# First stage of a one-core gMLP trunk: new load order, one chain of sums per tile, columns in one step

## The chip, the cores and the metric

The kernel runs on one core of one Trainium2 chip. The metric is the device time of one execution in microseconds (us); lower is better. A time of the profile is counted from the start of its span. TensorE is PE in the rows (PEld is its weight load), VectorE is DVE, ScalarE is ACT, GpSimd is POOL and SyncE, whose queue issues the DMAs, is SP.

## What is computed

The reference, for one sequence x of 2048 positions and 1024 channels and one conditioning vector c of 1024 (depth 1, expansion to 2048 channels):

```python
mod = silu(c) @ ada_w + ada_b                      # ada_w: 1024 x 3072
shift, scale, gate = split(mod, 3)
h = rmsnorm(x, norm_g) * (1.0 + scale) + shift
u, v, z = split(h @ w_in, 3)                       # each 2048 channels
u = gelu(u); v = layernorm(gelu(v), ln_g, ln_b)
v = einsum("hpq,bnqhc->bnphc", sp_w, v in chunks of 128) + sp_b
y = (u * v * silu(z)) @ w_out
out = rmsnorm(x + gate * y, final_g)
```

## The kernel before

Every large product is made of fp32r halves: an operand is split into hi (a copy rounded to fp32r, ACT, line 168) and lo (operand minus hi, DVE, line 169), and a product is three matmuls, hi·hi, hi·lo and lo·hi (mm3, lines 177 to 180). Sequences go in two blocks of 1024 positions; within a block the large products follow Strassen's scheme with seven half products p1 to p7, whose left sides are S[A11] to S[S4].

The change touches only the **first stage** (lines 723 to 831). It makes the normalised, modulated and transposed input of the first 512 positions, a1[0] to a1[7] (128 channels by 512 positions each), and multiplies it at once by the first columns of w_in: step k takes a1[k], splits it into sh and sl, and makes 18 matmuls of 128x512 into six PSUM banks: four row chunks of v (with ws[k][0], 512 columns) and two tiles of u (ws[k][1]). Steps 0 to 3 accumulate p1, steps 4 to 7 accumulate p2; between them the six banks are copied out by ACT (lines 489 and 326). All later stages follow this one on TensorE.

To modulate a1[k] the stage needs two columns per k, mscale and mshift. They come from ada_w: mod_load(j) (line 209) loads 128 columns of the shift part and 128 of the scale part as one tile aw of 128 x 2 x 8 x 128 values (1 MB, two DMAs of 512 KB, in pieces of 512 bytes), in three rotating buffers. mod_sum(j) (line 218) multiplies its eight k-slices by the eight columns of silu(c) (c_act) and adds them up in **two accumulators** am[:, 0] and am[:, 1], taken in turn: the first product of each is made by DVE (j = 0) or ACT (other j, line 225), six multiply-adds by DVE (line 229), and one more add brings the two together (line 232). Two matmuls with a column of ones then sum over the partitions (line 235, pm), and mod_cols (line 240) makes mscale and mshift with three small DVE instructions.

Ahead of the steps stands a **start**: SP loads c, norm_g and ada_b as rows (lines 724 to 731), then aw 0 and aw 1, then four chunks of x (512 KB each, lines 257 to 264), then wf 0 and wf 1 (the first w_in tiles, lines 272 to 282), aw 2 and wf 2. TensorE turns the rows into columns (line 733); ACT makes c_act (line 734). Each chunk of x is normalised: ACT squares and sums it (line 157), DVE makes the mean r_m (line 149), POOL its power (line 150), DVE multiplies (line 160); TensorE transposes it (line 782). In between TensorE runs products of the identity that nobody reads (spin, lines 751 to 754). Then a1[0] is modulated (line 253) and split, and the first product follows.

The order on DVE and ACT is the written one in the start and in the steps (manual_schedule, lines 769 and 791); TensorE's order is written in the start only, and left to the scheduler in the steps. In step k the program loads aw and wf of k+3, sums aw of **k+2**, modulates and splits a1[k], makes the columns of k+1, multiplies, and splits the weights of k+1 (lines 792 to 831): the sums run two steps ahead of their use. In step 4 it also loads the second half of x and two tiles for the next stage (lines 796 to 799).

## Time and profile before

| | |
|---|---|
| three timed runs | 1334.1, 1338.95, 1339.69 us; median 1338.95 |
| the profiled execution | 1334.47 us, of which its span is 1332.7 us |
| busy share of the span | PE 99%, DVE 81%, ACT 51%, POOL 2% |
| mean granted TensorE clock | 0.999 |
| first product of the steps | 22.06 us after the start of the span |
| last product of step 7 | at 59.91 us; the next stage's first product at 60.14 us |

The span is the time between the first and the last instruction; some 1.8 us of the execution lie around it. A busy PE is not a PE at its peak: matmuls are pipelined, and their ends are modelled.

### The profile page before, as it was taken

The numbers are of one execution on the slowest core, as the hardware profiler recorded it, in microseconds if no ns is written. First come the engines' busy times: TensorE is split into PE (matmuls) and PEld (weight loads), VectorE is DVE, ScalarE is ACT, GpSimd is POOL, SyncE is SP. The second block draws the span as 40 slices with busy tenths as digits, with TensorE's granted clock in tenths as the row PEclk, the third lists the DMA queues.
The fourth block names the chain that finished last, engine by engine and source line by source line (L and its number), as shares of the span: only waits on it lengthen the run. The fifth ranks groups of instructions, "written<-read, shape, count | busy, mean of one in ns | idle before, by whom it ended". The sixth has DMA issues, their size and how long they took to land.

```text
span 1332.7 us, 17438 instructions
## 1 busy us (share of the span) xinstructions
PE 1317.3 (99%) x6174; PEld 1097.6 (82%) x6174; DVE 1077.3 (81%) x1801; ACT 683.6 (51%) x1177; POOL 26.0 (2%) x42
## 2 busy tenths in 40 slices
PE   8999999999999999999999999999999999999997
PEld 7878887888888888788888888888888888888886
DVE  7889988888888988978678889887789944757975
ACT  5875454766755537634355545444544424344453
POOL 0000001000000000000000000000000000000101
PEclk9999999999999999999999999999999999999999
DMA  9871655555565648442243344433339622235723
GB/s 310 293 259 56 232 187 190 179 193 186 198 225 186 216 151 278 165 135 104 102 164 107 112 167 174 152 117 119 125 126 319 248 99 100 103 121 212 244 103 127
DMA packets 156800, 229.26 MB, mean 172 GB/s; under 512 B 9188, under 2 KB 91172, under 8 KB 153384
## 3 DMA queue, kind: packets, MB, share of 16 engines
q1 hardware_dynamic: 156712, 228.14, 50.1%
q8 instruction: 48, 0.79, 0.2%
q14 instruction: 40, 0.33, 0.1%
HBM read 160.47 MB, written 67.64 MB: 171 GB/s over the span
## 4 chain that ended last, share of the span: by engine, by line
PE 87%; DVE 6%; DMA 2%; issue 1%; ACT 1%; POOL 1%; SPq 0%; POOLq 0%; DVEq 0%; ACTq 0%
PE p_u L180 7%; PE p_u L179 7%; PE p_u L178 7%; PE p_z L179 7%; PE p_z L180 7%; PE p_z L178 7%; PE po L180 7%; PE po L179 7%; PE po L178 7%; PE p_v L178 6%; PE p_v L180 6%; PE p_v L179 6%; PE pmix_u L557 4%; DVE lo_p_v L169 1%; PE p L180 1%
## 5 line engine op out<-in xcount | busy, mean ns | idle before, releaser
L178 PE MATMUL p_v<-hi_p_v,sh 128*128 128x512 f32 x416 | 162.5, 391 | 1.9 <-DVE c_v L485 1.0
L180 PE MATMUL po<-hi_o,gl 128*128 128x512 f32 x416 | 162.1, 390 | 0.3 <-DVE gl L169 0.2
L179 PE MATMUL p_v<-lo_p_v,sh 128*128 128x512 f32 x416 | 162.3, 390 | 0.0
L180 PE MATMUL p_v<-hi_p_v,sl 128*128 128x512 f32 x416 | 162.2, 391 | 0.0
L178 PE MATMUL po<-hi_o,gh 128*128 128x512 f32 x416 | 161.8, 389 | 0.0
L179 PE MATMUL po<-lo_o,gh 128*128 128x512 f32 x416 | 161.8, 389 | 0.0
L168 ACT ACTIVATE gh<-gr 128x1024 fp32r<-128x1024 f32 x52 | 55.0, 1060 | 128.3 <-PE po L179 118.3
L168 ACT ACTIVATE hi_p_v<-b_v 128x512 fp32r<-128x512 f32 x104 | 64.9, 630 | 106.3 <-PE p_v L180 87.7
L169 DVE TENSOR_TENSOR gl<-gr,gh 128x1024 fp32r<-128x1024 f32 x52 | 63.5, 1221 | 59.8 <-ACT gh L168 59.7
L169 DVE TENSOR_TENSOR lo_p_v<-b_v,hi_p_v 128x512 fp32r<-128x512 f32 x104 | 69.7, 685 | 36.1 <-ACT hi_p_v L168 35.8
L178 PEld LDWEIGHTS p_v<-hi_p_v,sh 128*128 128x128 f32 x416 | 78.1, 188 | 19.5 <-DVE c_v L485 1.8
L180 PEld LDWEIGHTS po<-hi_o,gl 128*128 128x128 f32 x416 | 78.1, 188 | 17.2 <-DVE gl L169 1.1
L178 PEld LDWEIGHTS po<-hi_o,gh 128*128 128x128 f32 x416 | 78.1, 188 | 16.3
L179 PEld LDWEIGHTS po<-lo_o,gh 128*128 128x128 f32 x416 | 78.1, 188 | 16.2
L179 PEld LDWEIGHTS p_v<-lo_p_v,sh 128*128 128x128 f32 x416 | 78.1, 188 | 16.1 <-DVE lo_p_v L169 0.2
L180 PEld LDWEIGHTS p_v<-hi_p_v,sl 128*128 128x128 f32 x416 | 78.1, 188 | 16.0
L542 ACT ACTIVATE vn<-vn,lm,lr 128x256 f32<-128x256 f32 x128 | 67.7, 590 | 22.4 <-DMA vn<-v_dram 17.1
L180 PE MATMUL p_u<-sh,lo_p_u 128*128 128x512 f32 x196 | 76.3, 389 | 0.0
L178 PE MATMUL p_u<-sh,hi_p_u 128*128 128x512 f32 x196 | 76.3, 389 | 0.0
L179 PE MATMUL p_u<-sl,hi_p_u 128*128 128x512 f32 x196 | 76.2, 389 | 0.0
L180 PE MATMUL p_z<-sh,lo_p_z 128*128 128x512 f32 x192 | 75.0, 391 | 0.0
L178 PE MATMUL p_z<-sh,hi_p_z 128*128 128x512 f32 x192 | 74.7, 389 | 0.0
(248 smaller groups left out, 3113.0 us busy)
## 6 DMA issues: line engine op xcount, KB each, us to landing
gr<-g_dram SPq DMA_DIRECT2D x26, 1024.0 KB, 4.9
b_v<-in_gm_w_in_dram SPq DMA_DIRECT2D x18, 1024.0 KB, 7.5
vn<-v_dram SPq DMA_DIRECT2D x16, 1024.0 KB, 6.0
raw_u<-in_gm_w_in_dram SPq DMA_DIRECT2D x16, 1024.0 KB, 5.3
raw_z<-in_gm_w_in_dram SPq DMA_DIRECT2D x16, 1024.0 KB, 5.0
v_dram<-c_v SPq DMA_DIRECT2D x44, 256.0 KB, 2.1
g_dram<-c_u SPq DMA_DIRECT2D x37, 256.0 KB, 2.7
aw<-in_ada_w_dram SPq DMA_DIRECT2D x16, 512.0 KB, 5.4
```

Of the source, the lines that this page charges most:

```text
L168: nc.scalar.activation(hi, src, AF.Copy)
L169: nc.vector.tensor_tensor(lo, src, hi.bitcast(F32), op=ALU.subtract)
L178: nc.tensor.matmul(ps, lhsT=sh, rhs=mh, start=first, stop=False)
L179: nc.tensor.matmul(ps, lhsT=sh, rhs=ml, start=False, stop=False)
L180: nc.tensor.matmul(ps, lhsT=sl, rhs=mh, start=False, stop=last)
L542: nc.scalar.activation(vt[:, ch, :], vt[:, ch, :], AF.Identity, bias=lm[:, ch:ch + 1], scale=lr[:, ch:ch + 1],)
L557: nc.tensor.matmul(pm[:, i * P:(i + 1) * P], lhsT=vt[:, m * (NCH // 2) + i, f * P:(f + 1) * P], rhs=spT[:, u.j, :], start=True, stop=True,)
```

## The change

The rows are loaded behind aw 0, and x between aw 0 and aw 1; wf 0 comes ahead of aw 1. The sums of a tile run in one accumulator (one add on the other in place), the first product on ACT except for j = 1. The 1 of "1 + scale" is added once to all columns; mscale is then one DVE instruction, and mshift moves to ACT. The order is written out for three engines (DVE, ACT and PE) through the steps: in step k TensorE makes 8 products (13 in step 0), the column of k+1, four transposes (steps 1 to 3) and the other products; DVE adds the last four slices of aw k+1 (six in step 0) and the first three of aw k+2; ACT makes the upper halves of the weights of k+1 before it modulates a1[k+1]. All of a1[1] to a1[4] are copied by ACT. Spins: 6, 13, 3, 5, 4, 3, 6 and, in step 0, 5 more (before: 20, 16, 3, 3, 6).

```diff
@@ -215,38 +215,40 @@
             nc.sync.dma_start(aw[:, s], ada_v[:, :, s * D + j * P:s * D + (j + 1) * P])
         return aw
 
-    def mod_sum(j, aw):
-
-
-        am = s_slot(A22, j % KH, "hl"[j // KH], F32, f"am_{j}", (P, 2, 2, P))
-        for k in range(KD):
-            a, ck = am[:, k % 2], c_act[:, k:k + 1]
-            if k < 2 and j:
-                nc.scalar.activation(a, aw[:, :, k, :], AF.Copy, scale=ck)
-            elif k < 2:
-                nc.vector.tensor_scalar(a, aw[:, :, k, :], ck, None, op0=ALU.mult)
-            else:
-                nc.vector.scalar_tensor_tensor(a, aw[:, :, k, :], ck, a, op0=ALU.mult, op1=ALU.add)
-            if k in (3, 5, 6):
-                yield None
-        nc.vector.tensor_tensor(am[:, 0], am[:, 0], am[:, 1], op=ALU.add)
+    def mod_tile(j):
+        return s_slot(A22, j % KH, "hl"[j // KH], F32, f"am_{j}", (P, 2, P))
+
+    def mod_begin(j, aw, am):
+
+        ck = c_act[:, 0:1]
+        if j == 1:
+            nc.vector.tensor_scalar(am, aw[:, :, 0, :], ck, None, op0=ALU.mult)
+        else:
+            nc.scalar.activation(am, aw[:, :, 0, :], AF.Copy, scale=ck)
+
+    def mod_add(aw, am, ks):
+        for k in ks:
+            nc.vector.scalar_tensor_tensor(
+                am, aw[:, :, k, :], c_act[:, k:k + 1], am, op0=ALU.mult, op1=ALU.add
+            )
+
+    def mod_column(j, am):
+
         pm = aux_bank(f"pm_{j}")
         for s in (1, 0):
             nc.tensor.matmul(
-                pm[:, s:s + 1], lhsT=am[:, 0, s, :], rhs=ones[:, 0:1], start=True, stop=True
+                pm[:, s:s + 1], lhsT=am[:, s, :], rhs=ones[:, 0:1], start=True, stop=True
             )
-        yield pm
+        return pm
 
     def mod_cols(cols, j, pm):
-        nc.vector.tensor_tensor(
-            mscale[:, j:j + 1], pm[:, 1:2], cols[:, R_SC + j:R_SC + j + 1], op=ALU.add
+
+        nc.vector.tensor_scalar(
+            mscale[:, j:j + 1], pm[:, 1:2], cols[:, R_SC + j:R_SC + j + 1],
+            cols[:, R_G + j:R_G + j + 1], op0=ALU.add, op1=ALU.mult,
         )
-        nc.vector.tensor_scalar(
-            mscale[:, j:j + 1], mscale[:, j:j + 1], 1.0, cols[:, R_G + j:R_G + j + 1],
-            op0=ALU.add, op1=ALU.mult,
-        )
-        nc.vector.tensor_tensor(
-            mshift[:, j:j + 1], pm[:, 0:1], cols[:, R_SH + j:R_SH + j + 1], op=ALU.add
+        nc.scalar.activation(
+            mshift[:, j:j + 1], pm[:, 0:1], AF.Identity, bias=cols[:, R_SH + j:R_SH + j + 1]
         )
 
     def modulate(out, src, k):
@@ -281,8 +283,18 @@
         )
         return wv, wu
 
-    def first_split(k, raws):
-        return split_w(raws[0], f"wfv_{k}", (P, FB)), split_w(raws[1], f"wfu_{k}", (P, NF, P))
+    def first_upper(k, raws):
+
+        ws = []
+        for raw, shape, name in zip(raws, ((P, FB), (P, NF, P)), ("wfv", "wfu")):
+            hi = whp.tile(list(shape), F32R, tag="hi", name=f"hi_{name}_{k}")
+            lo = wlp.tile(list(shape), F32R, tag="lo", name=f"lo_{name}_{k}")
+            nc.scalar.activation(hi, raw, AF.Copy)
+            ws.append((hi, lo))
+        return ws
+
+    def first_lower(w, raw):
+        nc.vector.tensor_tensor(w[1], raw, w[0].bitcast(F32), op=ALU.subtract)
 
 
     class Unit:
@@ -721,74 +733,120 @@
     NU = len(units) // NB
 
     with tc.tile_pool(name="start", bufs=1) as st:
+        aws, wf, pm, am = {}, {}, {}, {}
+        aws[0] = mod_load(st, 0)
         nc.sync.dma_start(rows[R_C:R_C + KD, :], c.rearrange("o (k p) -> (o k) p", p=P))
-        nc.sync.dma_start(
-            rows[R_G:R_G + KD, :], norm_g.rearrange("o (k p) -> (o k) p", p=P)
-        )
         nc.sync.dma_start(
             rows[R_SH:R_SH + 2 * KD, :],
             ada_b[:, 0:2 * D].rearrange("o (k p) -> (o k) p", p=P),
         )
-        ps_r = aux_bank("ps_rows")
-        nc.tensor.transpose(ps_r[:, :NR], rows[:NR, :], ident[:NR, :NR])
-        nc.scalar.activation(c_act, ps_r[:, R_C:R_C + KD], AF.Silu)
-        nc.vector.tensor_copy(cols, ps_r[:, :NR])
-
-        aws, wf, pm = {}, {}, {}
-        for k in range(2):
+        nc.sync.dma_start(
+            rows[R_G:R_G + KD, :], norm_g.rearrange("o (k p) -> (o k) p", p=P)
+        )
+        xh = load_half(st, 0)
+        wf[0] = first_load(0)
+        for k in (1, 2):
             aws[k] = mod_load(st, k)
-        xh = load_half(st, 0)
-        for k in range(3):
-            if k == 2:
-                aws[k] = mod_load(st, k)
             wf[k] = first_load(k)
-        a1, first = [], []
+        a1, first, ws = [], [], {}
         firsts = [units[2 * j] for j in range(NF)]
         v0, v1 = groups[0]
-
         spun = acc_bank("spun")
 
-        def spin(n):
+        def spin(n, spun=spun):
 
             for _ in range(n):
                 nc.tensor.matmul(spun[:, :P], lhsT=ident, rhs=ident, start=True, stop=True)
 
...
+        def a1_tile(k):
+            a1.append(s_slot(S4, k % KH, "hl"[k // KH], F32, f"a1_{k}"))
+            return a1[k]
+
+        def upper(k):
+
+            if k:
+                modulate(a1[k], a1[k], k)
             else:
-                nc.scalar.activation(t, ps, AF.Copy)
-            a1.append(t)
-
-        written = {mybir.EngineType.DVE, mybir.EngineType.Activation}
-        with tc.manual_schedule(engines=written | {mybir.EngineType.PE}):
-            spin(20)
-            *_, pm[0] = mod_sum(0, aws[0])
+                modulate(a1_tile(0), psx[0], 0)
+            i, kk = (A11 if k < KH else A12), k % KH
+            hi, lo = [s_slot(i, kk, p, F32R, f"s{p}_0_{i}_{kk}") for p in "hl"]
+            S[i][kk] = (hi, lo)
+            nc.scalar.activation(hi, a1[k], AF.Copy)
+
+        def lower(k):
+            hi, lo = S[A11 if k < KH else A12][k % KH]
+            nc.vector.tensor_tensor(lo, a1[k], hi.bitcast(F32), op=ALU.subtract)
+
+        def products(k):
+            sh, sl = S[A11 if k < KH else A12][k % KH]
+            edges = k % KH == 0, k % KH == KH - 1
+            mm = []
+            for ch in range(4):
+                cs = slice(ch * P, (ch + 1) * P)
+                hi, lo = ws[k][0]
+                mm += [(first[ch], sh[:, cs], hi), (first[ch], sh[:, cs], lo),
+                       (first[ch], sl[:, cs], hi)]
+            for j in range(NF):
+                hi, lo = ws[k][1]
+                ps = first[4 + j]
+                mm += [(ps, hi[:, j], sh), (ps, hi[:, j], sl), (ps, lo[:, j], sh)]
+            for n, (ps, left, right) in enumerate(mm):
+                nc.tensor.matmul(
+                    ps, lhsT=left, rhs=right, start=edges[0] and n % 3 == 0,
+                    stop=edges[1] and n % 3 == 2,
+                )
+                yield
+
+        def some(steps, n):
+            for _ in range(n):
+                next(steps, None)
+
+        engines = {
+            mybir.EngineType.DVE, mybir.EngineType.Activation, mybir.EngineType.PE
+        }
+        with tc.manual_schedule(engines=engines):
+            spin(6)
+            ps_r = aux_bank("ps_rows")
+            nc.tensor.transpose(ps_r[:, :NR], rows[:NR, :], ident[:NR, :NR])
+            nc.scalar.activation(c_act, ps_r[:, R_C:R_C + KD], AF.Silu)
+            nc.vector.tensor_copy(cols, ps_r[:, :NR])
+            nc.vector.tensor_scalar(
+                cols[:, R_SC:R_SC + KD], cols[:, R_SC:R_SC + KD], 1.0, None, op0=ALU.add
+            )
+            spin(13)
+            norm = [normalize_steps(xt, f"0_{ch}") for ch, xt in enumerate(xh)]
+            am[0] = mod_tile(0)
+            mod_begin(0, aws[0], am[0])
+            mod_add(aws[0], am[0], range(1, 5))
+            next(norm[0])
+            mod_add(aws[0], am[0], range(5, KD))
+            next(norm[0])
+            pm[0] = mod_column(0, am[0])
             mod_cols(cols, 0, pm[0])
-            sums = mod_sum(1, aws[1])
+            next(norm[1])
+            next(norm[1])
+            next(norm[2])
+            next(norm[2])
+            ws[0] = first_upper(0, wf[0])
+            first_lower(ws[0][0], wf[0][0])
+            next(norm[3])
+            first_lower(ws[0][1], wf[0][1])
+            next(norm[3])
             psx = [acc_bank(f"psx_0_{k}") for k in range(5)]
             for ch, xt in enumerate(xh):
-                spin((16, 3, 3, 0)[ch])
-                norm = normalize_steps(xt, f"0_{ch}")
-                next(norm)
-                pm[1] = next(sums)
-                next(norm)
+                spin((3, 5, 4, 3)[ch])
                 for k in range(5):
                     nc.tensor.transpose(
                         psx[k][:, ch * P:(ch + 1) * P], xt[:, k * P:(k + 1) * P], ident
                     )
             spin(6)
-            ws = [first_split(k, wf[k]) for k in range(2)]
-            for k in range(5):
-                take_a1(k, psx[k])
-                if k == 0:
-                    put(0, A11, 0, a1[0])
-        with tc.manual_schedule(engines=written):
+            upper(0)
+            am[1] = mod_tile(1)
+            mod_begin(1, aws[1], am[1])
+            mod_add(aws[1], am[1], range(1, 2))
+            lower(0)
+            for k in range(1, 5):
+                nc.scalar.activation(a1_tile(k), psx[k], AF.Copy)
             for k in range(KD):
                 if k + 3 < KD:
                     aws[k + 3] = mod_load(st, k + 3)
@@ -797,38 +855,40 @@
                     x2 = load_half(st, 1)
                     v1.load(0, 0, "raw0")
                     v1.load(1, 0, "raw1")
+                if k % KH == 0:
+                    first = [acc_bank(f"p{k // KH + 1}_{j}") for j in range(4 + NF)]
+                mm = products(k)
+                some(mm, 8 if k else 13)
+                if k + 1 < KD:
+                    mod_add(aws[k + 1], am[k + 1], range(4 if k else 2, KD))
+                    ws[k + 1] = first_upper(k + 1, wf[k + 1])
+                    first_lower(ws[k + 1][0], wf[k + 1][0])
+                    pm[k + 1] = mod_column(k + 1, am[k + 1])
                 if k + 2 < KD:
-                    sums = mod_sum(k + 2, aws[k + 2])
-                    if k < 4:
-                        next(sums)
-                if k:
-                    modulate(a1[k], a1[k], k)
-                i = A11 if k < KH else A12
-                if k:
-                    put(0, i, k % KH, a1[k])
+                    am[k + 2] = mod_tile(k + 2)
+                    mod_begin(k + 2, aws[k + 2], am[k + 2])
+                if 0 < k < KH:
+                    ps = transpose_half(xh, 0, KH + k, aux_bank)
+                for _ in mm:
+                    pass
                 if k + 1 < KD:
                     mod_cols(cols, k + 1, pm[k + 1])
+                    first_lower(ws[k + 1][1], wf[k + 1][1])
+                    if k == 0:
+                        spin(5, aux_bank("spun_1"))
+                if k + 2 < KD:
+                    mod_add(aws[k + 2], am[k + 2], range(1, 4))
+                if k + 1 < KD:
+                    upper(k + 1)
                 if 0 < k < KH:
-                    take_a1(KH + k)
-                if k + 2 < KD:
-                    *_, pm[k + 2] = sums
-                if k == KH:
+                    nc.scalar.activation(a1_tile(KH + k), ps, AF.Copy)
+                if k + 1 == KH:
                     for ch in range(4):
                         v0.evict("p1", ch, first[ch])
                     for j in range(NF):
                         firsts[j].first(first[4 + j], None)
-                if k % KH == 0:
-                    first = [acc_bank(f"p{k // KH + 1}_{j}") for j in range(4 + NF)]
-                sh, sl = S[i][k % KH]
-                edges = k % KH == 0, k % KH == KH - 1
-                for ch in range(4):
-                    cs = slice(ch * P, (ch + 1) * P)
-                    mm3(first[ch], sh[:, cs], sl[:, cs], *ws[k][0], *edges)
-                for j in range(NF):
-                    hi, lo = ws[k][1]
-                    mm3(first[4 + j], hi[:, j], lo[:, j], sh, sl, *edges)
-                if 0 < k < KD - 1:
-                    ws.append(first_split(k + 1, wf[k + 1]))
+                if k + 1 < KD:
+                    lower(k + 1)
         right = [v1.weights("p1", k) for k in range(2)]
         for ch in range(4):
             v0.evict("p2", ch, first[ch])
```

## Rows read from the trace of the kernel before

**Rows 1.** The page: busy time of PE, and the chain that ended last.

```profile
PE 1317.3 (99%) x6174; PEld 1097.6 (82%) x6174; DVE 1077.3 (81%) x1801; ACT 683.6 (51%) x1177; POOL 26.0 (2%) x42
...
PE 87%; DVE 6%; DMA 2%; issue 1%; ACT 1%; POOL 1%; SPq 0%; POOLq 0%; DVEq 0%; ACTq 0%
```

**Rows 2.** Windows: steps 0, 1, 4, 7; length, busy us per engine, PEclk, DMA, GB/s.

```profile
core 0: us, PE busy (x) PEld busy (x) DVE busy (x) ACT busy (x) POOL busy (x), PEclk, DMA share, GB/s
22.00:28.05 6.05, 5.58 (x29) 4.14 (x29) 5.96 (x17) 4.02 (x9) 0.00 (x0) 1.00 1.00 300
28.05:33.09 5.04, 5.04 (x29) 4.21 (x28) 4.97 (x14) 3.67 (x7) 0.00 (x0) 1.00 1.05 313
...
42.80:47.35 4.55, 4.55 (x23) 3.85 (x22) 3.66 (x10) 4.52 (x10) 0.00 (x0) 1.00 1.03 410
...
56.06:60.14 4.08, 4.08 (x20) 3.38 (x18) 3.20 (x6) 3.19 (x5) 0.00 (x0) 1.00 0.41 159
```

**Rows 3.** Timeline of SP: start, length, issue, in the first 10 us.

```profile
0.74 0.40 SPq L724 DMA_DIRECT2D rows<-in_c_dram  x1
...
1.90 3.77 SPq L215 DMA_DIRECT2D aw<-in_ada_w_dram  x4
5.71 3.31 SPq L262 DMA_DIRECT2D x<-in_x_dram  x4
```

**Rows 4.** Windows of 1 us: the last figure is GB/s moved.

```profile
6.00:7.00 1.00, 1.00 (x7) 1.00 (x6) 0.00 (x0) 0.00 (x0) 0.00 (x0) 1.00 1.12 337
...
12.00:13.00 1.00, 1.00 (x12) 1.00 (x11) 0.00 (x0) 0.95 (x1) 0.00 (x0) 1.00 1.03 422
```

**Rows 5.** Timeline, 3 to 13 us: start, length, instruction, [idle before it].

```profile
3.15 0.28 PE L733 MATMUL ps_rows<-ident,rows 32*128 32x32 f32 x1 [3.15 <-DMA rows<-in_ada_b_dram]
...
3.36 7.34 PE L754 MATMUL spun<-ident 128*128 128x128 f32 x40
3.65 0.18 ACT L734 ACTIVATE c_act<-ps_rows 128x8 f32<-128x8 f32 x1
...
7.26 0.61 DVE L227 TENSOR_SCALAR am<-aw,c_act 128x256 f32<-128x256 f32 x2 [3.21 <-DMA aw<-in_ada_w_dram]
7.79 2.46 DVE L229 SCALAR_TENSOR_TENSOR am<-aw,c_act,am 128x256 f32<-128x256 f32 x6
...
10.28 0.42 DVE L232 TENSOR_TENSOR am<-am 128x256 f32<-128x256 f32 x1
...
10.76 0.61 PE L235 MATMUL pm<-ones,am 128*128 128x1 f32 x4
...
11.23 3.82 PE L754 MATMUL spun<-ident 128*128 128x128 f32 x32
11.40 0.16 DVE L241 TENSOR_TENSOR mscale<-pm,cols 128x1 f32<-128x1 f32 x1 [0.70 <-PE pm L235]
...
12.05 1.06 ACT L157 ACTIVATE sq<-x 128x1024 bf16<-128x1024 f32 x1 [8.23 <-DMA x<-in_x_dram]
```

**Rows 6.** Timeline, 13 to 23 us: chunks 0 and 3 of x, the first product.

```profile
13.24 0.15 DVE L149 TENSOR_SCALAR r_m<-ss 128x1 f32<-128x1 f32 x1 [1.36 <-ACT sq L157]
...
18.41 0.15 DVE L149 TENSOR_SCALAR r_m<-ss 128x1 f32<-128x1 f32 x1
...
19.39 0.75 DVE L160 TENSOR_SCALAR x<-x,r 128x1024 f32<-128x1024 f32 x1
...
22.06 0.49 PE L178 MATMUL p<-hi_wfv,sh 128*128 128x512 f32 x1
```

**Rows 7.** Timeline of DVE and ACT in the steps, 30 to 42 us.

```profile
30.81 0.80 ACT L253 ACTIVATE a<-a,mshift,mscale 128x512 f32<-128x512 f32 x1
30.89 0.69 DVE L169 TENSOR_TENSOR lo_wfv<-wfv,hi_wfv 128x512 fp32r<-128x512 f32 x1
...
31.49 0.42 DVE L169 TENSOR_TENSOR lo_wfu<-wfu,hi_wfu 128x256 fp32r<-128x256 f32 x1
...
31.64 0.63 ACT L168 ACTIVATE sh<-a 128x512 fp32r<-128x512 f32 x1
...
41.89 2.04 ACT L489 ACTIVATE c_v<-p 128x512 f32<-128x512 f32 x4
```

8 lines of the change are left out of this document (removed).

## The prediction

> **What bounds the kernel now.** I read the page first: TensorE is busy 99% of the span and carries 87% of the chain that ended last [rows 1]. After the first stage TensorE is the clock of everything, so a microsecond by which the stage ends earlier or later passes to the end. Then the windows by step [rows 2]: step 7 makes nothing but its 18 products, 4.08 us, so a product costs 0.227. Step 1, which also holds a column and four transposes, takes 5.04, step 4, with a column alone, 4.55; step 0 takes 6.05, with holes. DVE is busy 4.97 of the 5.04 us of step 1: it is as full as TensorE, and any DVE time added per step shows. Last the timelines: the stage has a start, in which TensorE does nothing useful, up to the first product at 22.06 [rows 6], and eight steps, up to 60.14 [rows 2].
>
> **The start.** Four edits move it.
>
> *Loads.* The first aw is issued at 0.74 instead of 1.90 [rows 3], 1.16 us earlier; the first sum waited for it until 7.26 [rows 5], so it lands near 6.1. Ahead of the first x chunk lies one aw tile less, 1.05 MB at 0.34 MB/us [rows 4], 3.1 us; the chunk was squared as it landed, at 12.05 [rows 5], so now at 12.05 − 1.2 − 3.1 = 7.8, and the next three 0.52/0.42 = 1.25 us apart [rows 4], the last at 11.6. Nothing below waits for them but chunk 0.
>
> *Rows of c, norm_g and ada_b* now queue behind that aw tile. They landed at 3.15, 2.4 us after the first of them was issued [rows 3, 5]. Not before 0.74 + 1.0 + 2.4 = 4.1, if the tile holds nothing up; not after chunk 0 at 7.8, behind which none of them stands. I take 6.1, with the tile: its packets are already in the same queue. The low end would gain only 0.3, as chunk 0 is waited for then; the high end costs 1.7.
>
> *Sums in one chain.* Before, two adds in a row touched different accumulators: six took 2.46 us at 0.48 for a single one, so one starts every 0.40. Where DVE needed what it had just written, it did not: the sum of the two accumulators begins at 10.28, 0.03 behind the end of the last add at 10.25 [rows 5]. So an add on the accumulator written just before costs 0.48 + 0.03 = 0.51, not 0.40; four in a chain last 3 × 0.51 + 0.48 = 2.0 us. The saved final add (0.42) is less than seven such waits (0.7). The Trainium skill (VectorE: DVE Perf Modes, section The DRAIN you can't avoid) says otherwise: the next instruction always waits until the pipe is empty, and eight copies took the same time with a wait behind each. By that rule the chain would cost nothing extra, and the sum would be that of rival B; the row shows adds that overlap by 0.08 where they are independent, and I go by the row.
>
> *Order.* c_act is ready at 6.1 + 0.5 + 0.2 = 6.8 (3.15 to 3.65, 0.18 long [rows 5]), the first product on ACT (taken as an add's 0.48) at 7.3, four adds at 9.3. The square of chunk 0 ends by 7.8 + 1.2 = 9.0 (12.05 to 13.24 [rows 5, 6]), so it is covered by the adds. Three more adds: 10.8. From the sum to mscale 0.70 (10.70 to 11.40 [rows 5]): 11.5; mshift, on ACT, 0.2 like mscale's kind: 11.7. ACT takes the squares of chunks 1 to 3 behind it, and this is the price of the written order: chunk 1 has lain there for 2.6 us. r_m of chunk 1 at 11.7 + 1.2 = 12.9. From r_m to the multiplication 0.98 (18.41 to 19.39), from there to the next r_m 0.67 [rows 6]: 14.5 for chunk 2; with a lower half of 0.60 (30.89 to 31.49 [rows 7]) put between, 16.8 for chunk 3, multiplied at 17.8. From there to the first product 2.67 (19.39 to 22.06 [rows 6]): **20.4, 1.65 us earlier**. The spins lie in TensorE's waits and cost nothing, while its clock holds (rival D).
>
> **The steps.** What is lost here is the lead. Before, aw k+2 was summed in step k, so the columns of k+1 lay ready when a1[k+1] was due. Now the last four adds of aw k+1, the column, mscale, mshift, the modulation, sh and sl follow each other within one step. I count from one sl to the next on DVE: sl 0.60, four adds 2.0, from there to mscale 0.70 (the lower half, 0.60, lies in that wait), mscale 0.15, the other lower half 0.34 (0.42 less the overlap [rows 7]), three adds 1.42 (2 × 0.51 + 0.40): **5.2 us**, against 5.04 and, in later steps, 4.55 for TensorE's load [rows 2]. The path through ACT, 0.60 + 2.0 + 0.70 + mshift 0.2 + modulation 0.83 (30.81 to 31.64) + sh 0.65 = 5.0 [rows 7], is nearly as long.
>
> - sl 0 to sl 1: six adds instead of four (+1.0): 6.2. The five added spins of step 0 fit into the idle time.
> - sl 1 to sl 4: 3 × 5.2 = 15.6.
> - sl 4 to sl 5: ACT first copies the last transposes (0.55) and the six banks (0.51 each, 41.89 on [rows 7]: 3.1), then two upper halves (0.85), the first product of aw 6 (0.45), mshift, modulation, sh (1.7): 6.6. Before, that first product came behind the split.
> - sl 5 to sl 6: 5.2. sl 6 to sl 7, without the three adds: 5.0.
> - from sl 7 to the end: 0.7, then 16 products at 0.227: 4.3.
>
> Sum: 20.4 + 6.2 + 15.6 + 6.6 + 5.2 + 5.0 + 4.3 = 63.3, against 60.14: the steps lose 4.8, the start gains 1.65, **+3.2 us**. The later aw loads wait longer for their buffers, but each still has some 4 us before its use; the moved bytes are the same. The one-step mscale and the shorter DVE work of the columns (0.15 for 0.4) are in the 5.2.
>
> Against the profiled execution: 1334.47 + 3.2 = 1337.7. That execution is one of the lower two of four (1334.1, 1334.47, 1338.95, 1339.69, mean 1336.8), 4.5 under the median shown. I predict from the mean: **1340.0**.
>
> **Rivals.**
>
> *A, the forecast* (chance 0.52): DVE's chain paces the steps. Its own range is +1.5 to +4.8 (bounds of the start, and waits that overlap by half a microsecond more), 1338.3 to 1341.6.
>
> *B, no price for the chain* (0.18). Adds follow at 0.40 whatever they touch: 0.5 less in the start, 0.7 in step 0, 0.5 over the next three (TensorE's 5.04 then binds), 0.5 and 0.3 later: 2.5 less, +0.7, 1337.5. Against it stands the 0.03 behind the end.
>
> *C, faster: TensorE alone paces the steps* (0.11), because ACT's and DVE's waits overlap better than I chain them. Steps: 5.3 (18 products, column, spins), 3 × 5.0, 3 × 4.5, 4.1, from 20.4: 58.3, −1.8, 1335.0. For it: before, TensorE waited little. Against it: DVE's own sum per step, without any wait, is 5.04.
>
> *D, slower: the clock* (0.06). Forty spin instructions took 7.34 us, thirty-two later ones 3.82, 0.18 against 0.12 each [rows 5]: I read it as a start at 1.2 GHz that rose to 2.4 during a stretch without a pause; in the steps the granted clock is 1.00 [rows 2]. The new start has a pause of some 3 us for the rows and others between the chunks. If the first steps ran at 1.2 GHz, 18 products would take twice 4.08 = 8.2 us, 3.0 more than a step of 5.2. It decides once two steps run so: +3.2 + 6.0 = +9.2, 1346.0. The Trainium skill (TensorE: Matmul & The Clock Gate, Part 1: The HAM clock gate) has it that the clock is throttled by default and that activity releases it; the spins between the chunks speak for a clock that holds.
>
> *E, x is not there earlier* (0.13), as the queue shares its rate otherwise than by order, or the rows land late: the start stays at 22.06, +4.8, 1341.6.
>
> **Chances and range.** About 0.5%, 6.7 us, is what a measurement of this kernel can tell from no change. Only D passes it upward, nothing passes it downward but scatter: faster 0.02, same 0.92, slower 0.06. Low end: C from the lowest run, 1334.1 − 1.8 = 1332.3. High end: E from the highest run, 1339.69 + 4.8 = 1344.5. Cases of both signs lie inside, but most of the chance says slower by a little.
>
> **What would show it.** Right, if the first product comes near 20.4; adds in a row start 0.51 apart; the distance between two sl is near 5.2 us in steps 1 to 3 and longest at step 4; ACT idles between the first sum and mshift 0 with x already landed; and the first product of the next stage stands near 63. Wrong, if adds start 0.40 apart; if TensorE's steps keep 5.0 and 4.5 us; if the first product comes before 19 or behind 22; or if products of the steps lie more than 0.227 apart in a row, which would be the clock.

## The result, and the profile after

The changed kernel takes 1343.1 us (median of seven runs, 1341.83 to 1348.23); seven runs of the kernel before beside it have a median of 1334.66. The ratio is 1.0066, 95% interval 1.005 to 1.0083: slower by 8 to 9 us. The profiled execution is one of 1341.83 us, span 1340.0, against 1334.47 and 1332.7.

The page of the changed kernel, its busy time and its chain, answers to [rows 1]:

```profile
PE 1318.8 (98%) x6168; PEld 1095.2 (82%) x6168; DVE 1079.6 (81%) x1783; ACT 684.6 (51%) x1180; POOL 25.8 (2%) x42
...
PE 85%; DVE 6%; ACT 3%; DMA 3%; issue 2%; POOL 1%; SPq 0%; POOLq 0%; DVEq 0%; ACTq 0%
```

TensorE does the same work. Two points of its share of the chain have gone to waits for ScalarE, DMA and issue. So the question is which waits.

The timeline of the changed kernel's start, 6 to 21 us, answers to [rows 5, 6]:

```profile
6.50 0.22 PE L810 MATMUL ps_rows<-ident,rows 32*128 32x32 f32 x1 [2.21 <-DMA rows<-in_norm_g_dram]
6.64 3.17 PE L759 MATMUL spun<-ident 128*128 128x128 f32 x26
...
7.37 1.06 ACT L157 ACTIVATE sq<-x 128x1024 bf16<-128x1024 f32 x1
7.50 2.05 DVE L231 SCALAR_TENSOR_TENSOR am<-aw,c_act,am 128x256 f32<-128x256 f32 x4
...
11.81 0.28 DVE L246 TENSOR_SCALAR mscale<-pm,cols 128x1 f32<-128x1 f32 x1
12.13 0.26 ACT L250 ACTIVATE mshift<-pm,cols 128x1 f32<-128x1 f32 x1 [3.60 <-DVE mscale L246]
12.29 1.05 ACT L157 ACTIVATE sq<-x 128x1024 bf16<-128x1024 f32 x1
...
20.69 0.49 PE L794 MATMUL p<-hi_wfv,sh 128*128 128x512 f32 x1
```

The first product comes at 20.69, 1.37 earlier than before. The four chained adds take 2.05 at 0.48 each, so one starts every 0.52. ScalarE starts to square chunk 0 at 7.37; the square of chunk 1 stands at 12.29, behind mshift 0, for which ScalarE idles 3.60 us: that is the written order.

The timeline of DVE and ACT in step 3, one whole round from sl to sl, answers to [rows 7]:

```profile
38.12 0.69 DVE L778 TENSOR_TENSOR sl<-a,sh 128x512 fp32r<-128x512 f32 x1
...
38.73 2.04 DVE L231 SCALAR_TENSOR_TENSOR am<-aw,c_act,am 128x256 f32<-128x256 f32 x4
...
40.69 0.68 DVE L297 TENSOR_TENSOR lo_wfv<-wfv,hi_wfv 128x512 fp32r<-128x512 f32 x1
...
41.47 0.28 DVE L246 TENSOR_SCALAR mscale<-pm,cols 128x1 f32<-128x1 f32 x1
41.67 0.41 DVE L297 TENSOR_TENSOR lo_wfu<-wfu,hi_wfu 128x256 fp32r<-128x256 f32 x1
41.78 0.26 ACT L250 ACTIVATE mshift<-pm,cols 128x1 f32<-128x1 f32 x1 [1.99 <-DVE mscale L246]
42.00 1.52 DVE L231 SCALAR_TENSOR_TENSOR am<-aw,c_act,am 128x256 f32<-128x256 f32 x3
42.08 0.81 ACT L255 ACTIVATE a<-a,mshift,mscale 128x512 f32<-128x512 f32 x1
42.92 0.63 ACT L774 ACTIVATE sh<-a 128x512 fp32r<-128x512 f32 x1
...
43.59 0.69 DVE L778 TENSOR_TENSOR sl<-a,sh 128x512 fp32r<-128x512 f32 x1
```

Read it as a loop that bites its own tail: sl, four adds, column, mscale, mshift, modulation, sh, the next sl: 0.61 + 1.96 + 0.78 + 0.31 + 0.30 + 0.84 + 0.67 = 5.47 us, start to start. mshift and mscale read the same tile of PSUM (pm), and mshift, on the other engine, starts 0.03 behind the end of mscale (41.75): the two are put in order. The trace names mscale as what released mshift: mshift waits for a semaphore that VectorE raises, so the order is a wait in the built program. No run shows what the chip would do without it. I had counted mshift as 0.2; from the start of mscale to the modulation it is 0.61.

Step 6 to 7, the timeline of DVE and ACT:

```profile
59.72 0.82 ACT L255 ACTIVATE a<-a,mshift,mscale 128x512 f32<-128x512 f32 x1
60.44 0.62 ACT L168 ACTIVATE hi_p_v<-b_v 128x512 fp32r<-128x512 f32 x1
60.96 0.61 ACT L774 ACTIVATE sh<-a 128x512 fp32r<-128x512 f32 x1
61.09 0.69 DVE L169 TENSOR_TENSOR lo_p_v<-b_v,hi_p_v 128x512 fp32r<-128x512 f32 x1 [1.37 <-ACT hi_p_v L168]
...
61.70 0.68 DVE L778 TENSOR_TENSOR sl<-a,sh 128x512 fp32r<-128x512 f32 x1
```

A weight split of the next stage has slipped between the modulation and sh, and its lower half ahead of sl.

| us | predicted | changed kernel |
|---|---|---|
| first product | 20.4 | 20.69 |
| sl 0 to 1 | 6.2 | 6.51 |
| sl 1 to 4 | 3 x 5.2 | 3 x 5.47 |
| sl 4 to 5 | 6.6 | 6.64 |
| sl 5 to 6, 6 to 7 | 5.2, 5.0 | 5.53, 5.94 |
| sl 7 to the next stage's first product | 4.3 | 4.50 |
| next stage's first product | 63.3 | 66.20 (before: 60.14) |

That is +6.06 us in the stage, not +3.2. If products of one name are matched between the two traces, counted back from the end, the lag is 6.2 to 6.5 from 70 to 260 us, 7.7 at 280 and 8.6 at 360; the rest of the loss arises there, in instructions that were not touched. At the last products it is 8.2. The span is only 7.3 longer, because behind its last product the kernel before takes 7.47 us in its trace and the changed one 6.63. Around 270 us (changed kernel, timeline of ACT, then the DMA view from the issue of that x chunk at 270.45 to its square):

```profile
276.94 1.06 ACT L157 ACTIVATE sq<-x 128x1024 bf16<-128x1024 f32 x1 [1.51 <-DMA x<-in_x_dram]
```

```profile
q1 hardware_dynamic: 2099, 2.36, 105.3%
q8 instruction: 1, 0.02, 1.0%
```

The same in the kernel before, from the issue at 264.27 (timeline of ACT; DMA view from 264.27 to 269.25):

```profile
269.25 1.06 ACT L157 ACTIVATE sq<-x 128x1024 bf16<-128x1024 f32 x1
```

```profile
q1 hardware_dynamic: 1250, 1.92, 104.6%
```

Before, ACT squared the chunk 4.98 us after its issue and did not wait; after, 6.49 us behind it, with a wait of 1.51. The view of the changed kernel is 1.5 us longer and so holds more packets of q1; over the first 4.5 us behind the issue the two are alike (1026 packets and 1.68 MB, before 1060 and 1.75). What the changed kernel's view has and the other lacks is a packet of q8, a queue of instructions.

### The profile page after: what moved, and what is told of

It reads as the page before. It is cut to its first block, busy times and chain, and to the rows that moved or that the text cites. A ratio compares the mean times of both kernels' runs of the same rounds, so it can differ in the third digit from the quotient of the medians.

```text
span 1340.0 us, 17416 instructions
## 1 busy us (share of the span) xinstructions
PE 1318.8 (98%) x6168; PEld 1095.2 (82%) x6168; DVE 1079.6 (81%) x1783; ACT 684.6 (51%) x1180; POOL 25.8 (2%) x42
## 4 chain that ended last, share of the span: by engine, by line
PE 85%; DVE 6%; ACT 3%; DMA 3%; issue 2%; POOL 1%; SPq 0%; POOLq 0%; DVEq 0%; ACTq 0%
PE p_z L180 7%; PE p_z L179 7%; PE p_z L178 7%; PE po L180 7%; PE po L178 7%; PE po L179 7%; PE p_u L179 7%; PE p_u L180 7%; PE p_u L178 7%; PE p_v L178 6%; PE p_v L180 6%; PE p_v L179 6%; PE pmix_u L569 4%; DVE am L231 1%; DMA x<-in_x_dram 1%
## 5 line engine op out<-in xcount | busy, mean ns | idle before, releaser
L168 ACT ACTIVATE gh<-gr 128x1024 fp32r<-128x1024 f32 x52 | 55.0, 1060 | 127.7 <-PE po L179 117.3
L169 DVE TENSOR_TENSOR gl<-gr,gh 128x1024 fp32r<-128x1024 f32 x52 | 63.5, 1222 | 59.7 <-ACT gh L168 59.6
```

Of the source, the lines that this page charges most:

```text
L168: nc.scalar.activation(hi, src, AF.Copy)
L169: nc.vector.tensor_tensor(lo, src, hi.bitcast(F32), op=ALU.subtract)
```

## The experiments

Theory A: the steps are paced by that loop, in which the lost lead of the sums put four adds of each tile, the column and mshift behind sl. Rival: VectorE's load alone paces them. Three of the first four expectations still call theory A "ScalarE's round"; it is put as a loop of dependences only in the one with one add more ahead, which tests it. "Stage end" is the next stage's first product, "sl to sl" the distance between the starts of two lower halves. Ratios are against the kernel before, run beside each. The intervals of the first three, single edits, overlap with the changed kernel's own, so what an edit is worth is read from the stage in its one trace.

**mshift on VectorE.**

```diff
-        nc.scalar.activation(mshift[:, j:j + 1], pm[:, 0:1], AF.Identity, bias=cols[...])
+        nc.vector.tensor_tensor(mshift[:, j:j + 1], pm[:, 0:1], cols[...], op=ALU.add)
```

> The column step of the changed kernel with mshift as an add on VectorE behind mscale, instead of an activation on ScalarE that waits for mscale's end. In the changed kernel one ScalarE round measured 5.47 us from lower half to lower half (sl to sl): mscale to modulate 0.61, modulate and upper half, then the evict, two more upper halves and the two first products of the sums. Theory A (ScalarE's round paces the steps, and mshift sits on it because it is put in order behind mscale, 0.3 to 0.4 us a step): sl to sl falls to some 5.3, the first product comes some 0.2 earlier (20.5), the first stage ends near 65.0 instead of 66.20, and the whole is about 1.2 us shorter than the changed kernel. Rival (VectorE's load paces): VectorE gets 0.07 us more work per step, sl to sl stays at 5.45 to 5.55, the stage ends at 66.0 to 66.8.

Measured: first product 20.58, sl to sl 5.37 to 5.41, stage end 65.20; 1.0043 (1.0028 to 1.0057). DVE and ACT of step 3:

```profile
41.11 0.28 DVE L246 TENSOR_SCALAR mscale<-pm,cols 128x1 f32<-128x1 f32 x1
41.31 0.15 DVE L250 TENSOR_TENSOR mshift<-pm,cols 128x1 f32<-128x1 f32 x1
41.37 0.41 DVE L297 TENSOR_TENSOR lo_wfu<-wfu,hi_wfu 128x256 fp32r<-128x256 f32 x1
41.49 0.82 ACT L255 ACTIVATE a<-a,mshift,mscale 128x512 f32<-128x512 f32 x1 [2.19 <-DVE mshift L250]
41.70 1.52 DVE L231 SCALAR_TENSOR_TENSOR am<-aw,c_act,am 128x256 f32<-128x256 f32 x3
42.34 0.63 ACT L774 ACTIVATE sh<-a 128x512 fp32r<-128x512 f32 x1
...
43.14 0.69 DVE L778 TENSOR_TENSOR sl<-a,sh 128x512 fp32r<-128x512 f32 x1
```

From mscale to the modulation 0.38 instead of 0.61, as theory A has it. But only 0.1 of the 0.23 reaches the step: sh ends at 42.97, and DVE goes straight from its three adds to sl at 43.14. Now DVE's own sum, 5.37, paces. The two limits lie within 0.15 us of each other.

**Two sums per tile.**

```diff
-    nc.vector.scalar_tensor_tensor(am, aw[:, :, k, :], c_act[:, k:k + 1], am, ...)
+    a = am[:, k % 2]
+    nc.vector.scalar_tensor_tensor(a, aw[:, :, k, :], c_act[:, k:k + 1], a, ...)
+    if k == KD - 1:
+        nc.vector.tensor_tensor(am[:, 0], am[:, 0], am[:, 1], op=ALU.add)
```

> The changed kernel with two running sums per tile again (two first products on ScalarE, six adds that don't depend on one another in pairs at 0.40, one add of the two halves at the end) instead of one chain of seven adds at 0.51. Theory A (ScalarE's round paces): what lies behind the lower half, four adds and the final one, is about as long as before, ScalarE gets another product of some 0.3 us per step; sl to sl stays at 5.45 to 5.8, only the start gains (first product some 0.4 earlier), and the stage ends at 65.2 to 67. Rival (VectorE's chain paces): VectorE loses 0.6 to 0.75 us per step, sl to sl falls to about 4.8, and the stage ends near 62.

Measured: first product 20.98, sl to sl 5.55 to 5.56, stage end 66.80; 1.0066 (1.005 to 1.0082). VectorE's load fell, and it idles in each round:

```profile
42.45 0.82 ACT L259 ACTIVATE a<-a,mshift,mscale 128x512 f32<-128x512 f32 x1
43.30 0.63 ACT L778 ACTIVATE sh<-a 128x512 fp32r<-128x512 f32 x1
...
43.97 0.69 DVE L782 TENSOR_TENSOR sl<-a,sh 128x512 fp32r<-128x512 f32 x1 [0.72 <-ACT sh L778]
```

The load is not what paces here. Behind sl stand four adds and the final one, 2.05 instead of 1.96, and the step grew by just that. The 0.4 expected in the start did not come: the first product was 0.29 later than in the changed kernel.

**The next stage's split behind the last halves.** One line is indented, so that it falls under the written order:

```diff
-        right = [v1.weights("p1", k) for k in range(2)]
+            right = [v1.weights("p1", k) for k in range(2)]
```

> The changed kernel with the splits of the next stage's right-hand tiles (hi_p_v on ScalarE, lo_p_v on VectorE, about 0.6 us each) written behind the last upper and lower half, where in the changed kernel they come ahead of them. Theory A (they sit in the last round's path): sl6 to sl7 falls from 5.94 to about 5.45 and the stage ends 0.5 to 0.9 earlier, 65.3 to 65.7, and the whole is as much shorter. Rival (the next stage needs them as early as that, so they are only moved): sl7 comes earlier, but the first products of the next stage start no earlier than now, 66.2.

Measured: sl 6 to 7 5.48, stage end 65.85 behind a first product 0.08 later than in the changed kernel; 1.0051 (1.0036 to 1.0066). The step gains 0.46 and nearly all of it reaches the end of the stage: theory A, though the stage's end lies just outside its 65.3 to 65.7.

**Both first edits.**

> Both edits together: mshift on VectorE and two sums per tile. Theory A (ScalarE's round paces, with mshift in it): about as with mshift alone, sl to sl 5.3 to 5.5, stage end 64 to 65.2. Rival (VectorE's chain paces): sl to sl about 4.8, stage end near 61.5 to 62. If neither paces alone but both are close, the two edits gain together more than the sum of the two alone.

Measured: sl to sl 5.33, stage end 64.90; 1.0029 (1.0015 to 1.0043). DVE in step 3:

```profile
37.49 0.69 DVE L782 TENSOR_TENSOR sl<-a,sh 128x512 fp32r<-128x512 f32 x1 [0.42 <-ACT sh L778]
38.10 1.67 DVE L233 SCALAR_TENSOR_TENSOR am<-aw,c_act,am 128x256 f32<-128x256 f32 x4
...
42.82 0.69 DVE L782 TENSOR_TENSOR sl<-a,sh 128x512 fp32r<-128x512 f32 x1 [0.43 <-ACT sh L778]
```

The loop with its parts, most of them as in the two runs above, gives 0.61 + 2.05 + 0.78 + 0.38 + 0.85 + 0.66 = 5.33. DVE's load here is that less the 0.43 us for which it idles, 4.9.

**One add more ahead of sl**, from the version with both edits; this is the direct test of the loop:

```diff
-  mod_add(aws[k + 2], am[k + 2], range(2, 4))
+  mod_add(aws[k + 2], am[k + 2], range(2, 5))
...
-  mod_add(aws[k + 1], am[k + 1], range(4 if k else 2, KD))
+  mod_add(aws[k + 1], am[k + 1], range(5 if k else 2, KD))
```

> The changed kernel with mshift on VectorE and two sums per tile, as in the earlier run of both (sl to sl 5.33, stage end 64.90), and one more add of the next tile written ahead of the lower half, so one less behind it. Theory (a loop of dependences sets the step: sl, the adds left, the column, mscale, mshift, modulation, upper half, next sl; each add written behind sl lies in it with its 0.41): sl to sl 4.9 to 5.05, where TensorE's own 5.04 binds, stage end 63.0 to 63.5. Rival (VectorE's load or ScalarE's paces, and an add moved from one side of sl to the other stays in it): 5.3, stage end 64.9.

Measured: sl to sl 4.93 to 4.97, stage end 62.25; 1.002 (1.0007 to 1.0033). DVE of step 2:

```profile
31.48 0.69 DVE L782 TENSOR_TENSOR sl<-a,sh 128x512 fp32r<-128x512 f32 x1
32.09 1.27 DVE L233 SCALAR_TENSOR_TENSOR am<-aw,c_act,am 128x256 f32<-128x256 f32 x3
33.40 0.42 DVE L237 TENSOR_TENSOR am<-am 128x256 f32<-128x256 f32 x1
...
34.56 0.28 DVE L250 TENSOR_SCALAR mscale<-pm,cols 128x1 f32<-128x1 f32 x1
...
36.45 0.69 DVE L782 TENSOR_TENSOR sl<-a,sh 128x512 fp32r<-128x512 f32 x1
```

The same instructions in another order: an add that crosses sl takes its 0.4 out of the step (5.33 to 4.95), and the stage ends before the 63.0 to 63.5 I expected. The rival is out for the version with both edits; the step now stands where DVE's load of 4.9 would put it too.

**The parts on the kernel before.** First its column step alone:

> The kernel before with the changed kernel's column step alone (mscale in one operation on a column to which 1 was added once, mshift on ScalarE, where it waits for mscale's end). Theory (the wait of mshift costs only where the columns are made within the step that needs them; in the kernel before they are ready a step earlier): VectorE saves some 0.25 us per step, ScalarE gets 0.26 us in a place where it waited 1.1 us for the transposes anyway: first product as before but some 0.25 later or earlier, stage end 60.14 minus 0 to 0.8, the whole within 1 us of before. Rival (the operation on ScalarE costs by itself, wherever it stands): 0.3 to 0.6 us for each of seven steps, stage end 62 to 64.

Measured: 0.9999 (0.9988 to 1.001). Steps 1 and 2 take 4.68 against 4.76, so the rival's 0.3 to 0.6 in every step is out; but the first product came at 22.89, 0.83 later, step 4 went from 5.79 to 7.32, and the stage ends at 62.21, not at 60.14 or ahead of it. ACT in step 4:

```profile
42.41 0.26 ACT L246 ACTIVATE mshift<-pm,cols 128x1 f32<-128x1 f32 x1 [0.95 <-DVE mscale L242]
42.77 0.91 ACT L225 ACTIVATE am<-aw,c_act 128x256 f32<-128x256 f32 x2
43.58 2.04 ACT L487 ACTIVATE c_v<-p 128x512 f32<-128x512 f32 x4
```

My expectation missed what stands behind the waiting instruction: six bank copies, which started at 41.89 before [rows 7] and now at 43.58. The whole stays level all the same. By matched products the lag is still 2.05 at 1200 us and 1.50 at 1300, and another 1.0 goes behind the last product (6.45 us to the end, 7.47 before); why, no run shows.

Then its chain of sums alone:

> The kernel before with the changed kernel's sums alone (one first product and a chain of seven adds per tile instead of two first products, six adds and a final one); order and lead of the sums as before. Theory (a dependent add starts 0.51 behind the one before it, and VectorE, busy 4.97 of 5.04 us, paces these steps): 3.5 us for a tile's adds instead of 2.8, so 0.6 to 0.75 more for each of steps 0 to 3, 0.2 to 0.5 for the two steps after, 0.4 in the start: stage end 63 to 64.5, the whole 3 to 4 us longer than before. Rival (the chain costs VectorE nothing that shows, since the price lies in the lost lead alone): stage end 60 to 61.

Measured: sl to sl 5.31 in steps 1 and 2 (before: 4.76), stage end 62.31; 1.0015 (1.0 to 1.0029). DVE has no pause in the round: the chain costs 0.55 a step where VectorE is full, a little under the 0.6 to 0.75 I expected, and nothing in step 3 (3.87, before 3.96). The stage's end lies between the two ranges, and the whole is 2 us longer, not 3 to 4.

**A version that might beat both.** The order of loads as changed; squares of all x chunks first on ScalarE; each r asked for ahead of the multiplication before it; half of sum 1 ahead of sl 0; three adds ahead; the split written last. The spins between the chunks go from 5, 4 and 3 to 2, 1 and 1.

```diff
-            pm[0] = mod_column(0, am[0])
-            mod_cols(cols, 0, pm[0])
-            next(norm[1])
-            next(norm[1])
-            next(norm[2])
-            next(norm[2])
-            ws[0] = first_upper(0, wf[0])
...
+            pm[0] = mod_column(0, am[0])
+            next(norm[1])
+            next(norm[2])
+            next(norm[1])
+            next(norm[3])
+            next(norm[2])
+            mod_cols(cols, 0, pm[0])
+            next(norm[3])
+            ws[0] = first_upper(0, wf[0])
...
+            mod_add(aws[1], am[1], range(2, 4))
```

> A version meant to beat both kernels: the changed kernel's order of loads, mshift on VectorE, two sums per tile, three adds ahead, the next stage's splits written behind the last lower half, and the start in another order: the squares of all four x chunks ahead of everything else on ScalarE, their multiplications as soon as their r is there, columns 0 and the split of the first weights behind them, and half of sum 1 ahead of the first lower half. Theory (in the changed kernel's start VectorE and ScalarE wait for one another by the written order while x has landed; the steps are the loop of dependences): first product at 16.5 to 17.5 instead of 20.69, then 5.0 to 5.6, three steps of 5.0, 6.1, 4.8 to 5.0 twice, stage end 57 to 58.5, the whole 2 to 3 us below before. Rival (the work that the start skips comes back in the steps, or the sums then wait for the loads of ada_w): first product early, but sl to sl 5.5 and more, stage end 60 or later, no gain over before.

Measured: first product 17.58, step 0 5.85, then 4.92 to 5.06, step 4 6.41, stage end 59.45, 0.7 ahead of before, but 0.95 behind the latest end I expected; the whole is 1.0009 (1.0 to 1.0018), no gain. More than the 0.7 is lost later: 1.5 us between 62 and 70, where TensorE waits for the second half of x to be normalised, 1.35 us at 270 and 2.1 between 300 and 360, at x chunks again.

**What lies at 270 us.**

```diff
-            spin(6)
+            spin(10)
```

> The changed kernel with four more spins ahead of the rows, in a stretch in which TensorE waits for them anyway (idle from 4.3 to 6.5 us). Two things are asked. First, what puts 1.3 us on the time near 270 us in the changed kernel and in all its variants, though the instructions there are the same as before. Theory (a load of instructions of 16 KB, which TensorE's stream calls for about every 257 instructions, falls between the issue and the landing of an x chunk, at 273.7 with the chunk issued at 270.45, and the chunk lands 1.2 to 1.5 us later for it; in the kernel before it ran at 262.1, ahead of the issue at 264.27; the changed kernel has 16 TensorE instructions fewer up to there): four spins are 16 instructions, the load comes ahead of the issue again, the chunk is squared about 5.0 us after its issue instead of 6.5, and the shift against before no longer grows by 1.3 us between 260 and 290: the whole 1.2 to 2 us shorter than the changed kernel. Rival (the chunk lands late for another reason, such as the order of the data in memory): squared 6.2 to 6.5 us behind the issue, as now. Second, the clock: with spins up to 6.3 us the pause is gone, and the 26 spin instructions behind the rows run at 0.12 us each, as in the changed kernel's profile, and not at 0.23, as in three of its variants.

Measured: the packet of instructions ran at 269.4, ahead of the issue at 271.80, and the chunk was squared 5.50 behind it; the chunk at 348.83 after 5.20 (changed kernel: 5.77). Between 260 and 290 the lag grows by 0.5 instead of 1.5. But 1.3 us of lag came in at 205 to 210 us, where DVE waits 3.9 us for a load of raw_u instead of 2.6, and the span, 1340.0, is that of the changed kernel. So the link holds at this chunk, and in this execution the time was moved as much as gained. The whole is 1.0047 (1.0034 to 1.0061), the median 1341.65 against 1343.1: the expected 1.2 to 2 us, but the intervals overlap. The 26 spins behind the rows took 3.17, as expected; the next version shows that the four more spins do not secure that.

> The version with the early start and the steps with three adds ahead (stage end 59.45, the whole 0.9 per mille over before), with twelve more spins in the start, four ahead of the rows and eight behind them, where TensorE waits. Theory (the load of TensorE's instructions that meets an x chunk near 265 and again near 344 us): 48 instructions move it ahead of both issues, the two chunks are squared about 5.0 us behind their issues instead of 6.3 and 6.65, and the whole is 1.5 to 3 us shorter than without the spins: 1334 to 1335.5, level with before or 1 us under it. Rival (no such link): 1337, unchanged. If the clock does not hold, 42 spin instructions at 0.23 end at 16.4 us and the first product comes 1 to 1.5 us later.

The edit: `spin(6)` to `spin(10)`, `spin(13)` to `spin(21)`. Measured: 1333.3 us, 0.9986 (0.9977 to 0.9994). DMA view of that chunk, from its issue at 264.31 to its square at 269.35:

```profile
q1 hardware_dynamic: 1264, 1.92, 103.7%
```

No packet of instructions any more, and 5.04 us from issue to square (without the spins 6.31); the later chunk took 5.20 instead of 6.65. The version with the same steps and without the spins had 1.0009, so they are worth 2 permille, although in this execution the spins ran at half rate for a while and the first product came 1.2 later, at 18.80. By matched products the 1.35 us at 270 become 0.1 and the 2.1 us between 300 and 360 become 0.5. Not all of the gain is that link: the 1.5 us between 62 and 70 don't arise either (TensorE idles 0.46 us there, in the kernel before 0.49), behind a stage that ends 1.0 later, at 60.42.

```diff
-        for ch, xt in enumerate(x2):
-            normalize_x(xt, f"0_{4 + ch}")
+        norm = [normalize_steps(xt, f"0_{4 + ch}") for ch, xt in enumerate(x2)]
+        for ch in (0, 1, 0, 2, 1, 3, 2, 3):
+            next(norm[ch])
...
                         v0.evict("p1", ch, first[ch])
+                    ws[k + 2] = first_upper(k + 2, wf[k + 2], (0,))
                     for j in range(NF):
                         firsts[j].first(first[4 + j], None)
+                    ws[k + 2] += first_upper(k + 2, wf[k + 2], (1,))
```

> The version with twelve more spins, and two orders changed: in the fourth step ScalarE makes the upper half of the next wide weights between the copies of the four wide and the two narrow banks instead of behind all six, and the second half of x is normalized with each square's r asked for one chunk ahead, as in the first half. Theory (VectorE's in-order wait for that upper half sits in the loop of step 4, sl to sl 6.41; and TensorE idles 2.4 us between 64 and 70 us because each multiplication of x waits 0.73 for its own r): sl 4 to sl 5 falls to 5.4 to 5.8, stage end 58.4 to 58.8, and the idle time of TensorE between 62 and 70 us falls to under 1.2: 1.5 to 2.2 us less than the version with spins alone. Rival for the first edit (TensorE then waits for the narrow banks instead): 6.1 and no gain; for the second (the planner of that stretch puts the operations back in its own order): idle time unchanged.

Measured: 1333.0 us, 0.998 (0.9971 to 0.999): faster than both kernels, by 2 permille against before. Against the version with spins alone (1333.3) it gains 0.3 us, not the 1.5 to 2.2 expected, and the intervals overlap: the runs don't show a gain from the two orders. First product 16.95, stage end 58.87. Windows from 62 to 70 us, this version and then the one without spins and orders:

```profile
62.00:70.00 8.00, 7.27 (x34) 4.96 (x34) 6.03 (x14) 7.03 (x14) 2.74 (x4) 1.00 0.83 272
```

```profile
62.00:70.00 8.00, 5.61 (x26) 3.38 (x25) 5.69 (x13) 5.64 (x12) 2.19 (x4) 1.00 0.23 89
```

TensorE's idle time there falls from 2.39 to 0.73 us, with a stage that ends 0.6 earlier. Step 4 did not gain: 6.39. mscale came 1.0 us earlier in its step, and then the modulation waited for what ScalarE had been given ahead of it, the upper half of the narrow weights and two first products. The gap to the version with spins alone in the stage (58.87 against 60.42) is there at the first sl already (17.23 against 18.78), and the steps are alike: it comes from the clock in the start.

## Why the prediction came out as it did

The time, 1343.1, lies inside the range, 1.4 us under its upper end, and 3.1 above the forecast. That it lies inside is in part luck. The forecast was a loss of 3.2 us, and the measured loss is 8.4 (1343.1 against 1334.66), more than the 4.8 at which my own range for rival A ended. It fits only because I set the upper end from the slowest of four times, 1339.69; and the forecast is as near as 3.1 because I started from their mean, 1336.8, 2.1 above the median of seven. I gave "within 0.5%" 0.92, and it is 0.66% slower. Of my signs of being right, the start, the spacing of the adds, the idle ScalarE and the longest step at step 4 came; the 5.2 was 5.47, and the next stage's first product stood at 66.20, not near 63.

- **The start** (20.4): 20.69. The rows landed later than assumed (6.50 for their transpose, 6.1 assumed), the chunk earlier (squared from 7.37, 7.8 assumed); the chain of r_m, multiplication and lower halves went as worked out, each part to 0.2 us. The first r_m of that chain came 0.6 late, half of it because mshift 0 stood behind mscale 0 here too.
- **The chain at 0.51**: as read from the 0.03 in [rows 5]: 2.04 for four, against 1.67 for four independent ones in the version with both edits. Adds of this shape, 0.48 long, start 0.40 apart where they are independent and 0.52 apart where each needs the one before. Rival B, no price, is out. The Trainium skill (VectorE: DVE Perf Modes, section The DRAIN you can't avoid) states that the next operation does not start until the pipe is empty, and adds that one that is not held starts earlier. The traces bear out the wait for the dependent adds and not for the independent ones.
- **The lost lead**: the right mechanism, shown by the run with one more add ahead.
- **The failed term** is the path through ACT, in which I counted "mshift 0.2" and nothing for mscale ahead of it, 5.0 in all. mshift waits for mscale, the pair costs 0.61, and the ACT path is 5.47. That is longer than DVE's own sum, which comes to some 5.32 in the changed kernel instead of 5.2 (column 0.78 for 0.70, mscale 0.20 for 0.15) and to 5.37 with mshift on it. Over the three distances from sl 1 to sl 4 the term costs 0.8 us, with sl 0 to 1 and sl 5 to 6 1.5. The sign stood in the trace of the kernel before, in the timeline of DVE:

```profile
3.86 0.19 DVE L735 COPY cols<-ps_rows 128x32 f32<-128x32 f32 x1 [2.83 <-ACT c_act L734]
```

  A copy of ps_rows waits for c_act on ACT to end, though both only read that tile.
- **sl 6 to 7** (5.0): 5.94. I did not ask what the planner would put between the written instructions once the written stretch ended; it costs 0.46 by the run that writes it last.
- **"the moved bytes are the same"**, so nothing later changes: that failed. The stage's end was to pass to the end of the kernel unchanged; some 2.4 us more were lost at the x chunks near 270 and 350 us. With spins added that move the packet, the loss at 270 us falls from 1.5 to 0.5 in the changed kernel and to 0.1 in the version with the early start; all thirteen traces, one of each kernel, agree that the chunk at 270 is late if the packet falls between its issue and its square, and not otherwise. For the chunk at 345 it is less clean: with the packet ahead of it the chunk still took 6.17 with the chain of sums on the kernel before and 5.56 with the column step on it. What made the rest of the lag there stays open.
- **Rivals C, D, E**: TensorE alone does not pace the steps; the clock cost no step (products in a row 0.23 apart); x was there earlier. That the loss of 8.4 comes near rival D's 9.2 is chance.

## What to carry to other kernels

When a value is made in the same step in which it is used, add up the closed loop from one use to the next, start to start, across all engines, and ask for each instruction in it whether it could stand on the other side of the loop's closing operation: with the same instructions, order alone made 5.33 or 4.95 us here. In these kernels two engines that read one PSUM tile are put in order by a wait in the built program, so a short reader moved to another engine to spare the first is not beside it but behind it. Before you explain a microsecond far from the edit, see where the loads of instructions fall.

## What the runs showed of the hardware

**Loads of instructions meet data on the DMA.** The page of the changed kernel counts 48 packets of 16 KB on q8 (packets, MB, share):

```profile
q8 instruction: 48, 0.79, 0.2%
```

With 12,336 matrix and weight-load instructions that is one per 257. The Trainium skill (Runtime: NRT & Kernel Launch, section Instruction fetch mechanics) states refills in 16 KiB blocks of 256 instructions and calls their cost mostly hidden: the trace agrees with the size and the distance. The cost does not stay hidden where a block meets a load that is waited for: at the chunk near 270 us the square stands 6.2 to 6.8 us behind the issue with the packet inside (the changed kernel, its five variants without spins, the first version of the early start) and 4.9 to 5.5 with it ahead (the kernel before, its two variants, all three with spins). Sixteen idle instructions in the start were enough to move the packet ahead of the issue, 270 us later. The chunk near 345 us, where two kernels were late without a packet inside, shows that this is not the only cause of a late chunk.

**The clock in the start.** The 26 spins behind the rows took 3.17 us in the changed kernel and 5.92 in the version with mshift on VectorE, which issues the same instructions on TensorE up to there; the first row is of PE there:

```profile
6.77 5.92 PE L759 MATMUL spun<-ident 128*128 128x128 f32 x26
12.48 0.57 PE L239 MATMUL pm<-ones,am 128*128 128x1 f32 x4
```

0.23 us each is about half the rate of 0.12, 1.2 against 2.4 GHz, though the profile's windows print a granted clock of 1.00 for both stretches. The trace's record of that clock has its first entry at 4.89 us in the one and at 12.62 in the other. Up to there the spins start 0.21 apart, behind it 0.11, and a window ahead of the first entry prints 1.00. In the changed kernel with nothing but the next stage's split written last the record begins at 4.47 and shows the fall itself, from 7.88 to 11.30, in the middle of the 26 spins, which start 0.11 apart ahead of it and 0.21 apart in it. Its window from 8 to 11.2 us, with the granted clock third from the end:

```profile
8.00:11.20 3.20, 3.20 (x17) 3.20 (x16) 3.02 (x9) 0.78 (x2) 0.79 (x1) 0.50 1.02 401
```

TensorE had spun from 1.36 to 4.29 and then waited 2.2 to 2.3 us for the rows in all three. With four more spins it spun to 6.0: two of the three versions that have them went on at the full rate (26 spins in 3.17 us, 42 in 4.96), the third at half of it until 10.5 (42 in 6.72). So the pause alone does not decide it; what does stays open.

In the version with mshift on VectorE the column came 1.3 us later and yet the first product did not (20.58): the path of the start lay with the normalization. In the two last versions it did lie with the spins: a first product at 16.95 behind 42 spins in 4.96 us, at 18.80 behind 42 in 6.72.
